# Fewer, longer stores and shorter middle loads in a scale-and-shift kernel that streams 33.7 MB

## The chip, the cores and the metric

The kernel runs on one core of one Trainium2 chip. Its time is the device time of one execution in microseconds (us). The profile's span, from the first to the last instruction, is some 1.8 us shorter.

## The reference

```python
batch, seq, dim = 32, 512, 256        # conditioning: 32 x 64, both projections: 64 x 256
gamma = conditioning @ gamma_proj
beta = conditioning @ beta_proj
return (x * (1 + gamma[:, None, :]) + beta[:, None, :]).astype(np.float32)
```

x and the result are 16.78 MB each, in float32. Everything else is small.

## The kernel before

Each of the 128 partitions holds 128 rows of 256 floats (1 KB a row, 128 KB in all), so the whole of x fits on chip. Loads are issued by SyncE, stores by ScalarE. `LOADS` and `STORES` say how the 128 rows of a partition are cut: each number of `LOADS` is one DMA of so many rows in every partition, each number of `STORES` the row at which one store ends.

```python
LOADS = {0: [8, 8, 8, 8, 32, 32, 26, 6]}
STORES = {0: (32, 64, 96, 112, 128)}
GROUP = 16
ON_DVE = 11
# ... loads of conditioning, gamma_proj, beta_proj on nc.scalar (3 DMAs)
for n in LOADS.get(s, [ROWS]):
    nc.sync.dma_start(out=xs[:, r : r + n, :], in_=x_v[s, :, r : r + n, :])
    r += n
# ... gamma and beta by TensorE into PSUM, a copy of them in SBUF
for r0 in range(0, ROWS, GROUP):
    v = xs[:, r0 : r0 + ON_DVE, :]            # 11 rows on VectorE
    w = xs[:, r0 + ON_DVE : r0 + GROUP, :]    # 5 rows on GpSimd
    # VectorE: v = (gamma + 1) * v, then v = v + beta
    # GpSimd:  w = w * gamma1,      then w = w + beta
    if s == 0 and r0 + GROUP == STORES[0][0]:
        nc.scalar.copy(out=held, in_=slabs[-1][:, ROWS - LOADS[SLABS - 1][-1] - 1, 0:1])
    for e0, e1 in zip((0,) + STORES[s], STORES[s]):
        if r0 < e1 <= r0 + GROUP:
            nc.scalar.dma_start(out=o_v[s, :, e0:e1, :], in_=xs[:, e0:e1, :])
```

The copy into `held` computes nothing that is wanted. It reads one element of the last but one load, so ScalarE, which issues the stores, waits there until nearly all of x has landed.

## Time and profile before

| what | value |
|---|---|
| time, median (range) of the 3 runs | 84.11 us (84.03 to 84.14) |
| span of the profile | 82.3 us |
| VectorE, GpSimd busy | 61%, 56% |
| two DMA queues, share of 16 engines | 48.3% + 48.2% |
| arithmetic on x | 11.65 to 60.94 us |
| last load landed / first store issued | 42.57 / 40.92 us |
| last store landed | 81.43 us |

The table is to be read from the bottom: the last store lands 20 us after the last arithmetic, so the arithmetic can slip without touching the end, and the DMA cannot.

### The profile page before, as it was taken

What the parts mean: (1) busy time and instruction counts of PE and PEld (TensorE: products, weight loads), DVE (VectorE), ACT (ScalarE), POOL (GpSimd) and SP (SyncE); (2) the same over time, 40 slices, a digit from 0 to 9 for tenths busy, and PEclk for the clock granted to TensorE, in tenths of its full rate; (3) what the DMA queues carried; (4) which work ended last, traced back from release to release, by engine and by line L of the source; (5) the groups of instructions that cost most, each with busy time, mean ns of one, the idle gap of its engine ahead of it and who ended that gap; (6) DMA issues with size and microseconds to landing.
All of it is one profiled execution on the core that took longest, in us unless ns stands there. A gap on an engine that the chain in (4) does not pass through costs nothing.

```text
span 82.3 us, 141 instructions
## 1 busy us (share of the span) xinstructions
PE 3.3 (4%) x8; PEld 2.1 (3%) x8; DVE 50.1 (61%) x23; ACT 2.1 (3%) x4; POOL 46.4 (56%) x22
## 2 busy tenths in 40 slices
PE   0050540000000000000000000000000000000000
PEld 0040500000000000000000000000000000000000
DVE  1040029999999999999999999999960000000000
ACT  0600030000000000000000000000000000000000
POOL 2000039999999999999999999999200000000000
DMA  2999999979989989999797996995996999889983
GB/s 44 347 423 422 430 410 542 478 335 462 510 351 414 510 382 386 440 440 466 312 569 319 510 494 271 510 510 255 510 510 271 494 510 398 367 382 486 406 382 128
DMA packets 2080, 33.69 MB, mean 410 GB/s; under 512 B 288, under 2 KB 416, under 8 KB 544
## 3 DMA queue, kind: packets, MB, share of 16 engines
q1 hardware_dynamic: 1152, 16.78, 48.3%
q10 hardware_dynamic: 928, 16.92, 48.2%
HBM read 16.92 MB, written 16.78 MB: 410 GB/s over the span
## 4 chain that ended last, share of the span: by engine, by line
DVE 52%; DMA 9%; issue 8%; PE 3%; ACTq 1%; ACT 1%
DVE xs L115 30%; DVE xs L118 23%; DMA gbproj<-in_beta_proj_dram 9%; PE gb_p L91 3%; ACTq L52 1%; ACTq L49 0%; ACT gb_s L95 0%; ACT gb_s L98 0%
## 5 line engine op out<-in xcount | busy, mean ns | idle before, releaser
L117 POOL TENSOR_TENSOR xs<-xs,gb_s 128x1280 f32<-128x1280 f32 x8 | 23.1, 2888 | 10.5 <-ACT gb_s L95 10.5
L115 DVE SCALAR_TENSOR_TENSOR xs<-gb_p,xs 128x2816 f32<-128x2816 f32 x8 | 24.7, 3085 | 5.8 <-ACT gb_s L98 5.8
L118 DVE TENSOR_TENSOR xs<-xs,gb_p 128x2816 f32<-128x2816 f32 x8 | 24.7, 3088 | 0.3
L119 POOL TENSOR_TENSOR xs<-xs,gb_s 128x1280 f32<-128x1280 f32 x8 | 23.1, 2885 | 0.6
L91 PE MATMUL gb_p<-gbproj,cond_T 128*128 128x256 f32 x4 | 2.0, 667 | 3.4 <-DMA gbproj<-in_beta_proj_dram 3.4
L79 DVE COPY wide<-cond_s 32x64 f32<-32x64 f32 x2 | 0.3, 182 | 2.9 <-DMA cond_s<-in_conditioning_dram 2.9
L81 PE MATMUL cond_T_p<-rident,wide 32*128 32x128 f32 x4 | 1.2, 456 | 4.5 <-DVE rident L69 4.5
L95 ACT ACT_TABLE_LOAD x1 | 1.3, 1283 | 2.4 <-issue 2.4
L91 PEld LDWEIGHTS gb_p<-gbproj,cond_T 128*128 128x128 f32 x4 | 1.2, 324 | 3.9 <-issue 3.7
L84 DVE COPY cond_T<-cond_T_p 128x128 f32<-128x128 f32 x2 | 0.6, 292 | 1.0 <-PE cond_T_p L81 0.9
L81 PEld LDWEIGHTS cond_T_p<-rident,wide 32*128 32x128 f32 x4 | 0.9, 317 | 4.5 <-DVE rident L69 4.5
L122 ACT COPY held<-xs 128x1 f32<-128x1 f32 x1 | 0.2, 191 | 28.9 <-DMA xs<-in_x_dram 28.9
L78 DVE MEMSET wide<- 32x128 f32 x2 | 0.3, 165 | 0.8 <-PEq L142 0.8
L95 ACT ACTIVATE gb_s<-gb_p 128x256 f32<-128x256 f32 x1 | 0.4, 384 | 7.5 <-PE gb_p L91 7.5
L98 ACT COPY gb_s<-gb_p 128x256 f32<-128x256 f32 x1 | 0.4, 367 | 0.0
masks.py:197 POOL MEMSET ident<- 32x32 f32 x1 | 0.1, 115 | 0.3 <-POOLq L142 0.3
masks.py:199 POOL TENSOR_SCALAR_AFFINE_SELECT ident<-ident 32x32 f32<-32x32 f32 x1 | 0.2, 203 | 0.1
L142 POOL MEMSET const-float32-0.0<- 128x1 f32 x1 | 0.1, 103 | 0.2 <-issue 0.2
L69 DVE COPY rident<-ident 32x128 f32<-32x128 f32 x1 | 0.2, 206 | 0.0
L142 POOL MEMSET const-bfloat16-1.0<- 128x1 bf16 x1 | 0.1, 107 | 0.0
L142 POOL MEMSET const-uint8-127<- 128x1 uint8 x1 | 0.1, 107 | 0.0
L142 POOL MEMSET const-float32-1.0<- 128x1 f32 x1 | 0.1, 103 | 0.0
## 6 DMA issues: line engine op xcount, KB each, us to landing
out_dram<-xs ACTq DMA_DIRECT2D x3, 4096.0 KB, 20.5
xs<-in_x_dram SPq DMA_DIRECT2D x2, 4096.0 KB, 24.6
xs<-in_x_dram SPq DMA_DIRECT2D x4, 1024.0 KB, 8.1
out_dram<-xs ACTq DMA_DIRECT2D x2, 2048.0 KB, 21.0
xs<-in_x_dram SPq DMA_DIRECT2D x1, 3328.0 KB, 35.2
xs<-in_x_dram SPq DMA_DIRECT2D x1, 768.0 KB, 35.0
gbproj<-in_gamma_proj_dram ACTq DMA_DIRECT2D x1, 64.0 KB, 6.3
gbproj<-in_beta_proj_dram ACTq DMA_DIRECT2D x1, 64.0 KB, 7.3
```

The lines of the kernel that those rows point to most:

```text
L52: nc.scalar.dma_start(out=gbproj[0::2, :], in_=gamma_proj)
L78: nc.vector.memset(wide, 0.0)
L81: nc.tensor.matmul(t_p, lhsT=wide.rearrange("b k h -> b (k h)"), rhs=rident, start=True, stop=True)
L84: nc.vector.tensor_copy(out=t_s, in_=t_p)
L91: nc.tensor.matmul(p_t[:, h * dim : (h + 1) * dim], lhsT=cond_T[h][:, s * P : (s + 1) * P], rhs=gbproj, start=True, stop=True)
L95: nc.scalar.activation(out=s_t[:, :dim], in_=p_t[:, :dim], func=mybir.ActivationFunctionType.Identity, bias=1.0, scale=1.0)
L98: nc.scalar.copy(out=s_t[:, dim:], in_=p_t[:, dim:])
L115: nc.vector.scalar_tensor_tensor(out=v, in0=rows(g_p, nv), scalar=1.0, in1=v, op0=ALU.add, op1=ALU.mult)
L117: nc.gpsimd.tensor_tensor(out=w, in0=w, in1=rows(g_s, nw), op=ALU.mult)
L118: nc.vector.tensor_add(out=v, in0=v, in1=rows(b_p, nv))
L119: nc.gpsimd.tensor_tensor(out=w, in0=w, in1=rows(b_s, nw), op=ALU.add)
L142: nc = _bacc.Bacc("TRN2", target_bir_lowering=False, num_devices=1)
```

## The change

Its intent is larger transfers where nothing is waiting (stores of 64, 48 and 16 rows, so runs of 64, 48 and 16 KB in each partition) and finer ones where arithmetic might wait (the two loads of 32 rows become four of 16).

```diff
-    LOADS = {0: [8, 8, 8, 8, 32, 32, 26, 6]}
-    STORES = {0: (32, 64, 96, 112, 128)}
+    LOADS = {0: [8, 8, 8, 8, 16, 16, 16, 16, 26, 6]}
+    STORES = {0: (64, 112, 128)}
```

## The prediction

> **What bounds the kernel now.** The kernel multiplies and adds over 16.78 MB, so I first asked whether an engine or the DMA is full. The page's first two parts and the DMA part answer it.
>
> ```profile
> span 82.3 us, 141 instructions
> PE 3.3 (4%) x8; PEld 2.1 (3%) x8; DVE 50.1 (61%) x23; ACT 2.1 (3%) x4; POOL 46.4 (56%) x22
> ...
> DMA  2999999979989989999797996995996999889983
> ...
> q1 hardware_dynamic: 1152, 16.78, 48.3%
> q10 hardware_dynamic: 928, 16.92, 48.2%
> HBM read 16.92 MB, written 16.78 MB: 410 GB/s over the span
> ```
>
> No engine is over 61%, but the two DMA queues together hold 48.3 + 48.2 = 96.5% of the 16 DMA engines' span. The digits of DMA dip below 9 because a packet is booked where it starts; they do not show real holes. To test that, I laid the trace's packet records side by side and counted the moments at which fewer than 16 packets were open. Between 2.4 and 80.5 us the missing engine time is 0.023 + 0.006 + 0.055 + 0.010 = 0.094 us as a mean over the 16 engines. The first x packet starts at 1.75 us, the last ends at 81.09 us, and the last store's semaphore is complete at 81.43 us. So the span is 2 us of start, 79 us of DMA without a hole, and 1.2 us of end.
>
> The chain of waits followed back from the last instruction names VectorE with 52%. That chain ends at 60.94 us with the last arithmetic and does not hold the 20 us of stores after it, so I don't take it as the bound. The timeline shows who has slack:
>
> ```profile
> 23.27 2.89 POOL L117 TENSOR_TENSOR xs<-xs,gb_s 128x1280 f32<-128x1280 f32 x1
> 24.11 3.08 DVE L115 SCALAR_TENSOR_TENSOR xs<-gb_p,xs 128x2816 f32<-128x2816 f32 x1
> ...
> 40.70 0.19 ACT L122 COPY held<-xs 128x1 f32<-128x1 f32 x1 [28.87 <-DMA xs<-in_x_dram]
> 40.92 20.43 ACTq L126 DMA_DIRECT2D out_dram<-xs  x5
> ...
> 52.30 2.89 POOL L117 TENSOR_TENSOR xs<-xs,gb_s 128x1280 f32<-128x1280 f32 x1
> 54.73 3.08 DVE L115 SCALAR_TENSOR_TENSOR xs<-gb_p,xs 128x2816 f32<-128x2816 f32 x1
> ...
> 57.85 3.09 DVE L118 TENSOR_TENSOR xs<-xs,gb_p 128x2816 f32<-128x2816 f32 x1
> ```
>
> The lines without brackets waited for no load: arithmetic starts when gamma and beta are ready (11.65 us) and then runs back to back to 60.94. The small copy `held` keeps every store back until the last but one load, the 26 rows, has landed. The copy starts at 40.70, the first store is issued at 40.92, and its first packets move at 41.81. Just then the last load (6 rows) is running out; its own packets end between 41.6 and 42.1. The handover from loads to stores is therefore nearly seamless already (the 0.055 us above).
>
> ```profile
> SPq L153 <- DMA out_dram<-xs: 38.7, 5, 9.7
> ```
>
> This line of the DMA queue's waits is the end of the program, standing for the five stores in turn. 38.7 us of stores in one row, the longest 9.7 us (4 MB), is full DMA speed.
>
> **What the Trainium skill says.** "DMA: Bandwidth & Descriptors", section "Where 436 GB/s comes from", gives the ceiling of the 16 ports as 435.2 GB/s. The trace agrees: a 4 MB store behind another lands 9.73 us after it, 4,194,304 / 9.73 = 431 GB/s. At most 1% is left to win by any layout of the same bytes.
>
> The same page, "Queues, rings and completion order", says that each DMA engine goes round-robin between its queues and changes only at packet boundaries. That makes a 64 KB run a coarser turn than a 32 KB one if loads and stores are open together. In this trace they are open together for some 0.3 us only.
>
> The same page, "Anatomy of one DMA — SWDGE (gpsimd) path", puts a fixed cost of about 2.0 us on each DMA, mostly completion latency. That is stated for the other way of issuing, and in this trace nothing of it shows on a DMA queued behind another: the two 2 MB stores land 4.88 and 4.87 us apart, half of 9.73. So I count no 2 us per DMA saved.
>
> **The change part by part.** The number of bytes, arithmetic instructions and DMAs stays: 8 + 3 + 5 = 16 DMAs before, 10 + 3 + 3 = 16 after. Each of the 16 DMA engines serves 8 of the 128 partitions, one packet per partition and DMA (the page's 2,080 packets are 1,824 of data and 16 x 16 semaphore writes of 9 ns).
>
> First, the price of a packet. From the landing marks: the first three stores (32 rows, 32 KB runs) land at 52.28, 61.95 and 71.68, the last load at 42.57, so (71.68 - 42.57) / 3 = 9.703 us per 32 rows. The 16-row stores land at 76.56 and 81.43, mean 4.875. Two 16-row stores cost 2 x 4.875 - 9.703 = 0.047 us more than one of 32 rows: 8 more packets per engine and one more semaphore write, some 5 ns per packet.
>
> Loads: two of 32 rows become four of 16. This adds 16 packets per engine and two semaphore writes: 2 x 0.047 = +0.094 us. It lies on the DMA's own path, so it counts in full. What it buys is rows 32 to 48 some 4.9 us earlier: the 32-row load lands at 23.05, 0.22 us before GpSimd takes it at 23.27. But nobody waits there, so it buys 0.
>
> Stores: 64 rows are two 32-row stores less one 0.047, 2 x 9.703 - 0.047 = 19.359. 48 rows are 9.703 + 4.875 - 0.047 = 14.531. With 4.875 for the last 16 the sum is 38.765, against 81.43 - 42.57 = 38.86 before: -0.095 us. The 64 KB and 48 KB runs are an extrapolation; no packet over 32 KB is in this trace.
>
> Are the larger stores ever late? The first needs rows up to 64, done at 36.45 (VectorE's fourth add, 33.36 + 3.09), and waits for `held` at 40.70 as now. It feeds the DMA to about 42.6 + 19.4 = 62.0. The second needs rows up to 112, done at 54.82 (51.73 + 3.09), 7 us early. It feeds to 76.5. The third needs the last add, 60.94, 15 us early. The wait for data is nowhere on the path.
>
> Are the loads late? Semaphores come round, so the sixth load waits to be issued for the conditioning to land (3.9 us), the seventh for the first load (5.47), the eighth for gamma (7.52); the new ninth and tenth should wait for beta (8.96) and for the second load (8.25). So all are issued by about 9.7 us. By then eight loads of 96 rows are queued, enough until about 32 us. No hole.
>
> Sum: +0.094 - 0.095 = 0.00 us. The 0.1 us by which the load phase lengthens moves `held` and the first store by as much; the shorter stores give it back.
>
> **The rivals.** (a) *Longer runs raise the DMA rate.* For it: 8 KB packets run 309 ns (26.5 bytes per ns), 32 KB ones 1,216 ns (26.9). Against it: the slope has flattened, and 16 packets saved per engine at 5 ns are 0.1 us. If larger runs brought the whole 0.9% between 431 and 435 GB/s to the 128 store rows, it would be 0.35 us: 83.7.
>
> (b) *Coarse turns delay the last load.* Where a 64 KB packet (estimate 2 x 1.216 = 2.43 us) gets in before the last 6 KB packets on some engine, the last load lands later: 42.57 + two turns of 2.43 = 47.4 us. Its rows are wanted by GpSimd at 52.30 and VectorE at 54.73. The bytes are the same, so nothing is lost: 84.1. Only five turns or more would reach the arithmetic, and even then the last store has 15 us of slack.
>
> (c) *Runs over 32 KB are slower*, through how 16 engines write in step to HBM or through a descriptor that has to be split. The skill's page lists, under "Latency and other measured facts", low rates for HBM copies with row pitches of 512 KiB and more. Here the pitch between partitions is 128 KB and does not change, and the 32 KB stores go at full speed. A slowdown of 3% on the 112 rows would add 1.0 us: 85.1. Nothing in the trace speaks for it, but nothing tests it either.
>
> (d) *Fewer completions save time each.* If each of the two DMAs taken from the stores had saved 2 us, it would be 80; the seamless landings (4.87 after 4.88) exclude that.
>
> **How the range and chances follow.** The predicted time is the one before, 84.1 us. The three runs before spread over 84.03 to 84.14, and my two terms of 0.09 may each be off by as much again. I take 83.8 to 84.5; the upper side is wider for the untested runs of (c). Faster by over 2% would need 82.4 us, which is more than the 1% left to the DMA's ceiling: 1%. Slower by over 2% (85.8) is (c) at twice the size assumed: 4%. Within 2%: 95%.
>
> **What would show it.** Of the changed kernel: load landings near 32.87 for the 64 to 96 rows and 40.8 for the 26 rows; `held` at about 40.8; stores landing 19.4, 14.5 and 4.9 us after one another; still about 1,824 data packets, mean 410 GB/s. A 64 KB packet over 2.5 us would prove (c); under 2.40 us, (a). A hole in the DMA between 42 and 81 us, an arithmetic instruction that waits for a load, or a last load landing after 52 us would prove a step of mine wrong.

## The result, and the profile after

| | median of 6 runs | range |
|---|---|---|
| before | 84.07 us | 83.95 to 84.48 |
| changed | 84.07 us | 84.00 to 84.19 |

The ratio is 0.9996, with a 95% interval of 0.9973 to 1.0018: the same time. Ratios here are the mean time of one kernel's fast runs over that of the other's of the same rounds, so they are not quite the ratio of the medians.

The page of the changed kernel, the parts that answer to those of before (span, DMA digits, queues with packets, megabytes and share):

```profile
span 82.3 us, 141 instructions
...
DMA  3899999999999999999999909999988888889983
...
q1 hardware_dynamic: 1440, 16.78, 48.7%
q10 hardware_dynamic: 640, 16.92, 47.8%
```

288 packets (256 of data, 32 semaphore writes) have moved from the stores' queue (q10) to the loads' queue (q1), and with them some of the share. A semaphore is the counter by which a DMA tells that it has landed. The sum is 96.5% as before. The 0 and the 8s among the digits are no holes: a 64 KB packet is booked in the slice where it starts, and one lasts longer than a slice.

The timeline (start, duration, engine, line, operation) at the places shown of before:

```profile
23.29 2.89 POOL L117 TENSOR_TENSOR xs<-xs,gb_s 128x1280 f32<-128x1280 f32 x1
...
40.90 0.19 ACT L122 COPY held<-xs 128x1 f32<-128x1 f32 x1 [29.05 <-DMA xs<-in_x_dram]
41.20 20.17 ACTq L126 DMA_DIRECT2D out_dram<-xs  x3
...
57.86 3.09 DVE L118 TENSOR_TENSOR xs<-xs,gb_p 128x2816 f32<-128x2816 f32 x1
```

The arithmetic stands where it stood, to 0.02 us. `held` and the first store are 0.2 to 0.3 us later. The DMA queue's own waits show the stores in turn:

```profile
SPq L153 <- DMA out_dram<-xs: 38.6, 3, 19.3
```

Three waits now, the longest 19.3 us for 64 rows, and a total of 38.6 instead of 38.7. So the stores take a little less; that the loads take a little longer shows in the later `held`.

For the finer comparison I use the trace's landing marks. Each DMA has 16 of them, one when each DMA engine has finished its share, and their mean is steadier than the last one. The start scatters from run to run: in all profiles taken, the rows up to 32 have landed at 13.07 to 13.34 us (mean). So I count from there. "Loads" is from that landing to the last load's, "stores" from there to the last store's, "tail" from the very last mark to the end of the span.

```
kernel              DMAs  packets/engine  loads   stores   sum    tail   waits left
before               16       114         29.24   38.96   68.20   0.83      1
changed              16       114         29.41   38.82   68.23   0.83      1
```

Packets are those of data; each is one partition's run of one DMA, as the trace records it. "Waits left" are the closing waits that have not been passed when the last store lands; experiments 1 and 9 to 11 are about them.

### The profile page after: what moved, and what is told of

It reads as the page before. It is cut to its first block, busy times and chain, and to the rows that moved or that the text cites. A ratio compares the mean times of both kernels' runs of the same rounds, so it can differ in the third digit from the quotient of the medians.

```text
span 82.3 us, 141 instructions
## 1 busy us (share of the span) xinstructions
PE 3.3 (4%) x8; PEld 2.1 (3%) x8; DVE 50.1 (61%) x23; ACT 2.1 (3%) x4; POOL 46.4 (56%) x22
## 3 DMA queue, kind: packets, MB, share of 16 engines
q1 hardware_dynamic: 1440, 16.78, 48.7%
HBM read 16.92 MB, written 16.78 MB: 409 GB/s over the span
## 4 chain that ended last, share of the span: by engine, by line
DVE 52%; DMA 9%; issue 8%; PE 3%; ACTq 1%; ACT 1%
DVE xs L115 30%; DVE xs L118 23%; DMA gbproj<-in_beta_proj_dram 9%; PE gb_p L91 3%; ACTq L52 1%; ACTq L49 0%; ACT gb_s L95 0%; ACT gb_s L98 0%
## 5 line engine op out<-in xcount | busy, mean ns | idle before, releaser
L122 ACT COPY held<-xs 128x1 f32<-128x1 f32 x1 | 0.2, 191 | 29.1 <-DMA xs<-in_x_dram 29.1
```

## The experiments

Twelve runs were made, in three calls of four; within a call they share the runs of the kernel before. All gave the correct result. None is 2% off the kernel before by the record's verdict (run 5 is "unclear", its interval reaching over 2%, the others "same"), so smaller differences are judged by the interval and the trace. Theory A, formed after the result from the packets' own durations, is: a packet takes the time of its bytes at 434 GB/s over 16 engines and 8 to 9 ns more, a semaphore write some 15 ns (A's own figure; the records of these writes last 7 to 9 ns), so parts of the change add and subtract. B is the 5 ns per packet of the prediction; C says that the layout plays no part.

| run | median us | ratio to before | 95% interval |
|---|---|---|---|
| 1 loads only | 84.61 | 1.0045 | 1.0031 to 1.0060 |
| 2 stores only | 84.17 | 0.9994 | 0.9980 to 1.0007 |
| 3 stores of 8 rows | 85.45 | 1.0144 | 1.0130 to 1.0158 |
| 4 loads of 8 rows | 84.87 | 1.0073 | 1.0061 to 1.0085 |
| before, same rounds | 84.22 | | |
| 5 first store of 80 rows | 85.73 | 1.0185 | 1.0169 to 1.0202 |
| 6 changed, no `held` | 84.80 | 1.0071 | 1.0051 to 1.0092 |
| 7 before, no `held` | 85.22 | 1.0121 | 1.0104 to 1.0139 |
| 8 fewest packets, 12 DMAs | 84.14 | 0.9994 | 0.9980 to 1.0008 |
| before, same rounds | 84.18 | | |
| 9 fewest packets, 16 DMAs | 83.99 | 0.9972 | 0.9959 to 0.9986 |
| 10 changed, 17 DMAs | 84.37 | 1.0021 | 1.0008 to 1.0033 |
| 11 stores only, 16 DMAs | 84.08 | 0.9982 | 0.9969 to 0.9995 |
| 12 changed again | 84.29 | 1.0008 | 0.9995 to 1.0021 |
| before, same rounds | 84.19 | | |

And the same table of landings as above, without runs 6 and 7, whose loads and stores overlap:

```
kernel              DMAs  packets/engine  loads   stores   sum    tail   waits left
1 loads only         18       130         29.42   38.89   68.31   1.06      5
2 stores only        14        98         29.24   38.84   68.08   0.95      3
3 stores of 8        28       210         29.42   39.87   69.29   1.08      5
4 loads of 8         20       146         29.75   38.90   68.66   1.08      5
5 first store 80     16       122         29.41   40.30   69.71   0.83      1
8 fewest             12        82         29.16   38.81   67.97   1.08      5
9 fewest, 16 DMAs    16       82.25       29.16   38.81   67.97   0.83      1
10 changed, 17 DMAs  17       114.1       29.41   38.81   68.22   0.99      4
11 stores, 16 DMAs   16        98.1       29.24   38.75   67.99   0.83      1
12 changed again     16       114         29.42   38.87   68.29   0.83      1
```

### 1. The loads of the change alone

```diff
-    LOADS = {0: [8, 8, 8, 8, 32, 32, 26, 6]}
+    LOADS = {0: [8, 8, 8, 8, 16, 16, 16, 16, 26, 6]}
```

> Loads of the change, stores of before: 16 more data packets and 2 more semaphore writes on each DMA engine than the kernel before. Theory A (a packet costs 8 to 9 ns over its bytes and a semaphore write some 15 ns, read from the packet records): last load landing near 42.75 us, end +0.17 us, 84.25. Theory B (the 5 ns per packet of the prediction): +0.09 us, 84.15. Theory C (the packets' size plays no part and the equal times are chance): +0.00.

The time was 84.61 us, +0.38 beside 84.22, twice what A gave. The trace splits it. The load stage is 29.42 against 29.24 us: +0.18, which is A (+0.17), and not B or C. The stores come out 0.07 us shorter than before with the same packets, part of it a handover with 0.02 instead of 0.06 us of idle engine time. The rest is in a place where neither theory looked: from the last landing to the end of the span are 1.06 us instead of 0.83. The DMA queue's waits tell why. All five stores now stand behind one wait:

```profile
SPq L153 <- DMA out_dram<-xs: 48.5, 1, 48.5
```

and when that is over, SyncE still walks through its other closing waits, though all that they wait for has landed. The view of the program's last line shows when SyncE gets to its closing drain (count, durations in ns, first and last start), first of the changed kernel:

```profile
L153 SPq DRAIN  x3: 7/7/7, 81.5 to 81.8; - x3
```

and the same view of this run:

```profile
L153 SPq DRAIN  x3: 7/7/7, 81.9 to 82.2; - x3
```

The last stores landed at 81.46 and 81.57 us, 0.11 apart; the drains begin 0.4 us (81.54 and 81.88, 0.34) apart. So I formed theory E, which runs 9 to 11 test: the program has eight DMA semaphores, handed out to its DMAs in turn, and waits for them at the end in a fixed order, some 60 ns a wait. The trace has six such waits for the eight semaphores, nearly in the order of handing out: for the third; the fourth and the second; the fifth and the first; the sixth; the seventh; the eighth. When the number of DMAs is a multiple of eight, the last store has the last semaphore, and one wait is left when it lands. With 18 DMAs it has the second, and five are left, its own included; the other four start at 81.63, 81.69, 81.75 and 81.81 us.

### 2. The stores of the change alone

```diff
-    STORES = {0: (32, 64, 96, 112, 128)}
+    STORES = {0: (64, 112, 128)}
```

> Loads of before, stores of 64, 48 and 16 rows: 16 fewer packets and 2 fewer semaphore writes per engine than before. A: from the last load's landing to the last store's 38.69 us instead of 38.86, end -0.17 us, 83.9. B: -0.095 us, 83.97. C: 84.07.

84.17 against 84.22 us: -0.05 by the medians, and by the ratio no difference can be shown. The trace again has the gain and the place where it went. Stores take 38.84 instead of 38.96 us (-0.12; A said -0.17, B -0.095), the sum is -0.12, and the tail is 0.12 us longer, with three waits left after 14 DMAs. The two cancel. What blurs the stores' part is the handover from loads to stores, whose idle engine time (mean, between 40 and 45 us) differs from profile to profile: 0.06 us before, 0.10 in the changed kernel, 0.12 here, 0.04 in run 11, 0.16 in run 12. Without it the stores take 38.90 us before and 38.70 to 38.72 in these four: -0.18 to -0.20, which speaks for A.

### 3. The changed kernel with stores of 8 rows

```diff
-    STORES = {0: (64, 112, 128)}
+    STORES = {0: (16,) + tuple(range(24, 129, 8))}
```

> The changed kernel with its stores cut into one of 16 rows and fourteen of 8: 15 stores for 3, 96 more packets and 12 more semaphore writes per engine. A: +1.0 us, 85.05. B: +0.56 us, 84.6. Rival D (each DMA costs some 2 us of its own on the path): +24 us, 108. C: no change.

The store stage grew by 39.87 - 38.82 = 1.05 us for 96 packets and 12 semaphore writes per engine, which is A's +1.0 and twice B's +0.56. That is 0.087 us for eight packets and one semaphore. The time was 85.45 us, 1.23 above before. Beside the profile of before the loads are 0.18, the stores 0.91 and the tail 0.25 us longer, 1.34 in all; the execution profiled before took 84.04 us, 0.18 below the 84.22 of these rounds. Rival D, some 2 us per DMA, is far off: twelve more DMAs would have added 24 us.

```profile
out_dram<-xs ACTq DMA_DIRECT2D x14, 1024.0 KB, 16.4
```

This line of the DMA issues (count, KB each, us to landing) fits that: a store waits 16.4 us from issue to landing, nearly all of it in the queue, so any fixed latency can pass behind the stores ahead.

### 4. The changed kernel with middle loads of 8 rows

```diff
-    LOADS = {0: [8, 8, 8, 8, 16, 16, 16, 16, 26, 6]}
+    LOADS = {0: [8] * 12 + [26, 6]}
```

> The changed kernel with its four middle loads of 16 rows cut into eight of 8: 32 more packets and 4 more semaphore writes per engine. A: last load landing some 0.33 us later (43.1 us), 84.4. B: +0.19, 84.25. C: no change. If it is more than 0.5 us, the loads' issue starves on semaphores that come round.

Loads took 29.75 us against 29.41: +0.34, as A has it. Four DMAs of eight packets each cost 0.085 us apiece, nearly the price of the stores in run 3. The time was 84.87, so +0.65 beside before: 0.5 of it in loads (29.75 - 29.24), 0.25 in the tail (five waits left), with the stores giving back a little. The wait for semaphores that come round did not starve the loads.

### 5. A first store of 80 rows

```diff
-    STORES = {0: (64, 112, 128)}
+    STORES = {0: (80, 112, 128)}
```

> The changed kernel with stores of 80, 32 and 16 rows. Rows up to 80 are done at 42.59 us, 1.4 us after the first store is issued now. Theory (the DMA is the bound, and the first store's data have 4.7 us of slack at 64 rows but are late at 80): first store issued near 42.75, its first packets at 43.6, a hole of some 1.4 us in the DMA, 85.5. Rival (larger runs win the time back, or the store's start isn't on the path): 84.1. The 80 KB run may be split; the trace will tell the size of its packets.

85.73 us, +1.55. The timeline has the first store at the time foretold:

```profile
41.02 0.19 ACT L122 COPY held<-xs 128x1 f32<-128x1 f32 x1 [29.19 <-DMA xs<-in_x_dram]
42.64 18.71 ACTq L126 DMA_DIRECT2D out_dram<-xs  x3
```

Between the copy and the issue ScalarE waits for the fifth group of rows. The DMA has a hole of 1.50 us (mean over the 16 engines, between 40 and 45 us), where the changed kernel has 0.10. The store stage grew by 40.30 - 38.82 = 1.48 us: 1.40 of the hole, and the rest is about what eight more packets per engine cost. So the start of the first store is on the path, and a hole there comes out at the end in full. The packets of this store are 40 KB, two per partition: an 80 KB run was split in two.

### 6. The changed kernel without the copy that holds the stores

```diff
-                    nc.scalar.copy(out=held, in_=slabs[-1][:, ROWS - LOADS[SLABS - 1][-1] - 1, 0:1])
+                    pass
```

> The changed kernel without the small copy that holds the stores back: the first store goes out near 36.5 us and its 64 KB packets take turns with the 26 KB and 6 KB ones of the last two loads. If coarse turns cost no DMA time: load 9 lands near 47 and the last load near 61 us, the arithmetic ends near 67 instead of 61, and the time stays 84.0 to 84.2, because the bytes are the same and the last store's rows are still ready before the DMA wants them. If mixed turns cost rate or the late load reaches the end: 85 or more.

84.80 us, ratio 1.0071: between the two expectations. The late load came, later still than foretold (64.2 us instead of 61; the 26 rows came earlier, 43.6 instead of 47):

```profile
64.21 3.09 DVE L115 SCALAR_TENSOR_TENSOR xs<-gb_p,xs 128x2816 f32<-128x2816 f32 x1 [9.30 <-DMA xs<-in_x_dram]
64.26 2.89 POOL L117 TENSOR_TENSOR xs<-xs,gb_s 128x1280 f32<-128x1280 f32 x1 [11.77 <-DMA xs<-in_x_dram]
```

The last group waits 9.3 us on VectorE and 11.8 on GpSimd, and its store is issued at 70.50 instead of 61.03 us. The DMA did not want it before some 76 us, so that costs nothing: the mean landing of the last store, counted from the rows up to 32, is 68.21 us, against 68.23 for the changed kernel. What costs is the spread: 15 of the 16 engines finish between 81.25 and 81.73 us and one at 82.29, and the last one counts (in the changed kernel all finish within 0.20 us). One mark is late already when the first store lands: 15 lie between 61.63 and 62.13 us, one at 62.93. The mixed turns, one 64 KB packet of a store for one 6 KB packet of the load over some 22 us, don't explain it: in them every 64 KB packet took 2,418 to 2,424 ns and every 6 KB packet 234, with next to no idle time. But just before, 12 load packets of 26 KB that started between 39.2 and 39.6 us took 1.07 to 1.95 us instead of 0.99; the first store packet started at 40.33. So mixed turns of 64 KB took no DMA time here, and the engine most likely became late at the moment where the stores began. The packet records don't name the engine, so that the longest of these packets made it late is not shown.

### 7. The kernel before without that copy

The same edit, on the kernel before.

> The kernel before without that copy: the first store of 32 rows goes out near 24.3 us, so loads and stores are open together for some 35 us, in turns of 32 KB each. If mixing costs nothing, the DMA stays full and the time is 84.1; if reading and writing in turns costs rate, it shows here most: 85 or more, with packets longer than 1,216 ns.

85.22 us, ratio 1.0121. Here both happen: the spread is 0.77 us instead of 0.25 (again one engine, 0.36 us behind the other 15), and the mean is 68.64 instead of 68.20 us, so 0.44 us are lost on average too. The long-packet sign is mixed: the stores' 32 KB packets are at 1,213 ns and the loads' median is 1,216, but single loads reach 2,761 ns and their mean is 1,269 instead of 1,218. The trace shows where these are: 25 load packets of 1.38 to 2.76 us, all started between 25.8 and 28.0 us, after the first store's issue (24.34) and before its first packet (29.10). In the 37 us of turns that follow (29.1 to 66) there is none. Summed, the long packets cost each engine 0.82 us here and 0.24 in run 6, and the other packets, a little shorter than with the copy, give back 0.32 and 0.20. That makes +0.50 and +0.04, against +0.44 and -0.02 in the mean landings. So the mean loss, too, arises where the stores begin among the loads, and not in the turns. Why load packets get long there, and more of them here than in run 6, stays open.

### 8. The fewest packets

```diff
-    LOADS = {0: [8, 8, 8, 8, 16, 16, 16, 16, 26, 6]}
+    LOADS = {0: [8, 8, 16, 32, 58, 6]}
```

> The changed stores with loads of 8, 8, 16, 32, 58 and 6 rows: 32 fewer packets and 4 fewer semaphore writes per engine than the changed kernel. A: -0.33 us, 83.75. B: -0.19, 83.88. The 58-row load lands near 40.5, so the arithmetic on rows 64 to 80 starts at 40.5 instead of 34.9 and ends near 67 us; rows up to 112 are then done near 60.7, just before the first store runs out near 61.7. If it comes late, the DMA has a hole there and the gain is lost.

84.14 us, ratio 0.9994: the gain expected is not in the time. Counted from the rows up to 32, the sum is 67.97 us, 0.26 less than the changed kernel's (A for the 24 packets and three semaphores after that point: 0.25). There is no new hole: rows up to 112 are ready and their store is issued at 59.28 us, before the first store is through at 61.7. The gain is in the tail, which is 1.08 us with five waits left. This was the miss that made me test theory E.

### 9. The fewest packets, and 16 DMAs

Run 8 with these lines after the loads of x:

```diff
+    pad = consts.tile([1, 4 * cond_dim], f32)
+    for i in range(4):
+        nc.sync.dma_start(out=pad[:, i * cond_dim : (i + 1) * cond_dim], in_=conditioning[i : i + 1, :])
```

> Loads of 8, 8, 16, 32, 58 and 6 rows and the changed stores, 12 DMAs, plus 4 loads of one run of 256 bytes that nobody reads, so 16 DMAs. Theory E (the eight DMA semaphores are handed out in turn and the closing waits stand in a fixed order of some 61 ns each, so that after 16 DMAs only one wait is left when the last store lands, after 12 five): 0.83 us from the last landing to the end instead of 1.07, 0.24 us less than with 12 DMAs; beside the kernel before -0.3 us, ratio 0.9965. Rival (the longer end is the chip's scatter): ratio 0.999 as with 12 DMAs. The four loads may add some 0.1 us on one DMA engine.

83.99 us, ratio 0.9972, interval 0.9959 to 0.9986. The four needless loads made the kernel faster: the tail is 0.83 us, one wait left, and the sum is unchanged at 67.97. The DMA queue's waits show it: the stores are waited for three times, as in the changed kernel, and not twice as in run 8. So does the drain, which begins at 81.5 us after a last landing at 81.42; in run 8 it began at 81.66 after 81.33.

```profile
SPq L157 <- DMA out_dram<-xs: 35.5, 3, 19.5
...
L157 SPq DRAIN  x3: 7/7/7, 81.5 to 81.8; - x3
```

### 10. The changed kernel with 17 DMAs

The same lines with 1 for 4, on the changed kernel.

> The changed kernel with one load of one run of 256 bytes that nobody reads: 17 DMAs. E: the last store's semaphore stands three waits earlier, four waits after the last landing instead of one: +0.18 us, 84.25 to 84.3. Rival (the longer end is scatter, or only the work on the DMA counts): +0.02.

84.37 us, ratio 1.0021, against 1.0008 for run 12 of the same rounds: +0.11 us. The tail has 0.99 us and four waits left, +0.16, which is E's +0.18 nearly. By the times alone the two intervals overlap, so here the trace carries the verdict.

### 11. Stores of the change, loads of before, 16 DMAs

The same lines with 2 for 4, on run 2.

> Loads of before, stores of 64, 48 and 16 rows, and two loads of one run of 256 bytes that nobody reads: 16 DMAs instead of 14. E: one wait after the last landing instead of three, so -0.12 us beside the same without them; beside the kernel before -0.15 us, ratio 0.998. Rival: as with 14 DMAs, ratio 0.9995.

84.08 us, ratio 0.9982, interval 0.9969 to 0.9995, as E has it (0.998), and the tail is 0.83 again. So the stores' part of the change is worth 0.15 us by the ratio (0.0018 of 84.2), once the number of DMAs is put right.

### 12. The changed kernel once more

Nothing edited; it stands beside runs 9 to 11.

> The changed kernel unchanged, for the same rounds as the three others: 16 DMAs, ratio 1.000 within 0.001.

84.29 us, ratio 1.0008, interval 0.9995 to 1.0021: the same as before once more. Run 9 is 0.9972 / 1.0008 = 0.9964 of it, 0.3 us faster. Run 9 beats both kernels, if only by this much.

## Why the prediction was right

The time on record, 84.1 us, is within 0.03 us of the measured one, and the mechanism is the one it gives: a full DMA, the same bytes, packets moved from stores to loads.

- *The DMA is the bound and has no holes.* Shown. Its idle time between 2.4 and 80.4 us is 0.13 us in the changed kernel, 0.09 before. Run 5 made a hole of 1.5 us and the end came 1.55 us later. Run 6 delayed the last arithmetic by 9.5 us and the mean landing did not move.
- *Loads +0.094 us.* Right in kind, too small: +0.17 in the changed kernel, +0.18 in run 1. The term that was mis-sized is the 0.047 us for eight packets and a semaphore. It came from the last marks of a few stores, which land 9.67 to 9.73 us apart, and its three 32-row stores include the 0.056 us of idle time in the handover. With the mean marks, and without that idle time, the same trace gives 2 x 4.890 - 9.707 = 0.073. Runs 3 and 4 measure 0.087 and 0.085.
- *Stores -0.095 us.* The same term: -0.14 in the changed kernel, -0.12 in run 2, and -0.18 to -0.20 without the handover's idle time (run 2).
- *The sum is 0.00.* Right because both terms used the same price and the change moves 16 packets one way and 16 the other. A wrong price could not spoil it.
- *The numbers named beforehand.* The load of rows 80 to 96 landed at 32.97 (32.87 said), the 26 rows at 40.88 (40.8), `held` ran at 40.90 (40.8), and the stores landed 19.37, 14.46 and 4.86 us after one another (19.4, 14.5, 4.9).
- *Rivals (a) and (c), longer runs faster or slower.* Both out: a 64 KB packet took 2,424 ns at the median, 2,430 being the estimate. It is two of 32 KB less one overhead of 8 ns.
- *Rival (b), coarse turns.* Out for the changed kernel, whose last load landed at 42.77 us. Forced in run 6, it leaves the mean landing as it was, as the prediction has it, but one engine late, which the prediction had not thought of, and costs 0.7%.
- *Rival (d), 2 us per DMA saved.* Out, run 3.

One thing the prediction missed and was lucky in. It counted 16 DMAs on both sides and took that for a count of semaphore writes only. Because 16 is a multiple of eight on both sides, the tail is the same. Either half of the change alone has 18 or 14 DMAs and pays 0.23 or 0.12 us at the end.

## What to carry to other kernels

Where the DMA has no hole, first ask what the change does to bytes, to the number of packets and to the start of the DMA's work; here finer loads and coarser stores at full rate were only an exchange of packet overheads (some 0.085 us for eight packets per engine and a semaphore write). A gain of some tenths of a microsecond can go astray in the last microsecond: look at how many closing waits are left when the last store lands. And a needless transfer or a hold-back copy may be worth its price: here some 0.2 us for the four loads of run 9 beside run 8, and 0.6 and 1.0 us for the copy that keeps the stores from starting among the loads (runs 6 and 7).

## What the Trainium skill lacked or had wrong

- "DMA: Bandwidth & Descriptors", Bandwidth and Anatomy: its fit, made for the other way of issuing, has some 2.0 us for each DMA. The page gives a packet's overhead in cycles, but no price for a DMA that is queued behind others. Here that price is 0.085 to 0.087 us for eight packets per engine and one semaphore write (runs 3 and 4); a packet of 32 KB takes 1,216 ns, of 64 KB 2,424 ns.
- The same page, "Where 436 GB/s comes from": it says that between HBM and SBUF the HBM's share of about 358 GB/s binds, though it also lists a single core at 425. With one core running, the stores here went at 16.78 MB / 38.82 us = 432 GB/s, close to the port ceiling of 435.2 and well over that share.
- The same page, "Queues, rings and completion order": it puts some 9 to 17 descriptors into the packet that an engine drains before it changes queues, and has no time for a second queue's first turn. In runs 6 and 7 a turn was one packet of the trace, one partition's run: 64 KB for 6 KB, 32 KB for 32 KB. In run 6 the first store packet started 3.71 us after its issue and in run 7 4.76 us, against 0.88 us where the loads were nearly out (before). The second queue waited some three packets of the first longer; that these were already taken by the engine is my inference.
- None of the pages has, as far as I looked, a program's own closing waits (what the runtime adds around a kernel is listed, these are not): some 60 ns for each closing wait that is left when the last DMA lands, and 0.83 us from that landing to the end of the span when only one is left. With eight semaphores in turn, 16 DMAs leave one wait, 17 four, 14 three, 12, 18, 20 and 28 five.
- No page that I read has what happens where stores begin among loads, that load packets get long and one engine finishes late: without the hold-back copy the 16 engines finish over 1.04 and 0.77 us (runs 6 and 7) and a 32 KB packet took up to 2.76 us; with it they finish over 0.16 to 0.35.
